# Up projection by seven products: sums of weights moved from GpSimd to accumulating transfers and VectorE, six plain pairs first

## The chip, the cores and the metric

The kernel runs on one core of one Trainium2 chip. It is a single program that computes all three blocks of the reference. The metric is device time in microseconds, the median of several runs. A core has five instruction queues: PE (TensorE, matrix products; PEld is its weight load), DVE (VectorE), ACT (ScalarE), POOL (GpSimd) and SP (SyncE, which here only issues transfers). Each works through its own instructions in order and waits on semaphores of the others.

## The reference

The input is x, 512 positions of 1024 features, fp32. Three blocks follow: an even mixer (differential attention and a chunked mLSTM), an odd mixer (spatial gating) and, after 16 meta tokens are put in front, a hybrid mixer (convolution and stick-breaking attention) with a gated feed-forward network. The change lies in the feed-forward network alone:

```
def conv_gated_mlp(xn, w_up_gate, conv_w_ffn, w_down):
    u, g = jnp.split(xn @ w_up_gate, 2, axis=-1)     # 1024 -> 2 x 2816
    u = causal_dwconv_2(u, conv_w_ffn)               # three taps over positions
    return (jax.nn.gelu(u) * g) @ w_down             # 2816 -> 1024
```

u and g are 2816 columns each, that is 22 blocks of 128 columns. Block m of u and block m of g make "pair" m; `act[m]` is gelu(conv(u)) * g of that pair.

## The kernel before, in words

Every fp32 operand of a product is split into a high part in fp32r and the remainder (hi by a cast on ACT, L77; lo by a subtraction on DVE, L78), and each product is three matmuls, hi*hi, hi*lo, lo*hi (`mm3`, L103 to L105). A weight block of 128 columns is loaded by one transfer on SP's queue (`load_w`, 512 KB, tile `wraw`, three buffers) and split into `whi` and `wlo` (three buffers each).

The up projection runs over the 22 pairs. The first `FIRST` pairs are plain: u and g are each 8 blocks of the inner dimension by two halves of 258 (or 254) positions, so 2 x 2 x 8 x 3 = 96 matmuls for a pair. Meanwhile the normalised input is combined for the later pairs: `xn` (L1367), the four sums `tq` (`seven_x`) and their split `sxh`, `sxl`.

The other pairs use a scheme of seven products (Strassen and Winograd): the weights of u and g, the two halves of the inner dimension, and the two halves of the positions make a 2 x 2 by 2 x 2 block product, done with 7 block products in place of 8, so 7 x 4 x 3 = 84 matmuls of 258 columns. `seven_w` forms the sums of weight blocks (`sa`, `sb`), `seven` issues the products into four PSUM tiles (`ps_sx`, `ps_sy`, `ps_sz`, `ps_sw`), keeps some of them in SBUF (`sn`, L173) and combines them to u and `act`. `conv_gelu` then applies the three taps (L1340, twice L1342), gelu (L1344), and POOL multiplies (L1377).

`residual` transposes the residual stream back to tokens (PE transposes `ps_h`, then four copies `ht` each on DVE); eight such calls are written into pairs 6 to 13, but a scheduler decides where they stand. The down projection follows (`ps_d`), whose input splits (`xl<-act`) may stand in the up projection already.

The program is put in order by a scheduler with a cost model of its own; the order on each engine is then fixed. It is the order that the chip runs, so it is shown below as it was built. In PE's order the pairs follow each other; only four matmuls of the first two products of pair m+1 stand ahead of the last two products of pair m.

Of the kernel before, what the change touches and what calls it, by code (L numbers as in the profile page):

```python
# [8 lines left out]
F32 = mybir.dt.float32  # L9
F32R = mybir.dt.float32r  # L10
BF16 = mybir.dt.bfloat16
AF = mybir.ActivationFunctionType
# [22 lines left out]
def kernel(ctx: ExitStack, tc: tile.TileContext, a, out):  # L35
# [84 lines left out]

    HK = KT // 2

    def add(o, x_, y_, op=ALU.add, eng=None):
        return (eng or G).tensor_tensor(o, x_, y_, op=op)

    def seven_w(pool, r1, r2):

        sa = pool.tile([128, KT, 128], F32, tag="sa", name="sa", bufs=4)  # L130
        sb = pool.tile([128, KT, 128], F32, tag="sa", name="sb", bufs=4)
        lo, hi = slice(0, HK), slice(HK, KT)
        add(sb[:, lo], r2[:, lo], r2[:, hi])
        add(sa[:, lo], sb[:, lo], r1[:, lo], ALU.subtract)
        add(sa[:, hi], r1[:, lo], r2[:, lo], ALU.subtract)
        add(sb[:, hi], r1[:, hi], sa[:, lo], ALU.subtract)
        w = {}
        for raw, names in ((r1, "12"), (sa, "67"), (sb, "53"), (r2[:, hi], "4")):
            sp_ = split_w(raw)
            for i, nm in enumerate(names):  # L140
                w[nm] = [x_[:, i * HK:(i + 1) * HK] for x_ in sp_]
        return w

    def seven_x(pool, tmp, p, xa, xb, n, out):

        tq = tmp.tile([128, 4, n], F32, tag="tq", name="tq")
        h0, h1 = slice(0, n), slice(n, 2 * n)
        t1, t2, t3, t4 = (tq[:, i] for i in range(4))
        add(t1, xa[:, h1], xa[:, h0], ALU.subtract)
        add(t3, xb[:, h1], xa[:, h1], ALU.subtract)  # L150
        add(t2, xb[:, h1], t1, ALU.subtract)
        add(t4, xb[:, h0], t2, ALU.subtract)
        for src, names in ((xa[:, h0], "1"), (xb, "23"), (tq.rearrange("p a b -> p (a b)"), "5674")):
            sp_ = [pool.tile([128, n * len(names)], F32R, tag=f"sx{names}{r}{p}", name=f"sx{r}") for r in "hl"]
            split(src, *sp_)
            for i, nm in enumerate(names):
                out[nm, p] = [x_[:, i * n:(i + 1) * n] for x_ in sp_]

    def seven(sw, sx, n, snp, o11, o12, o21, o22):

        bank = {}

        def product(nm, b, start):
            if start:
                bank[b] = pst("mm", n, f"ps_s{b}")
            wh, wl = sw[nm]
            for k in range(HK):
                mm3(bank[b], wh[:, k], wl[:, k], *sx[nm, k], start and k == 0, k == HK - 1, **kw)
            return bank[b]

        def keep(ps):
            t_ = snp.tile([128, n], F32, tag="sn", name="sn", bufs=5)
            A.copy(t_, ps)  # L173
            return t_

        s1 = keep(product("1", "x", True))
        add(o11, product("2", "y", True), s1, eng=V)
        u2 = keep(product("6", "x", False))
        s7 = keep(product("7", "w", True))
        u4 = keep(product("5", "x", False))  # L180
        add(o12, product("3", "z", True), u4, eng=V)
        n22, n21 = o22.shape[1], o21.shape[1]
        add(o22, u4[:, n - n22:], s7[:, n - n22:])
        add(o21, product("4", "w", False)[:, n - n21:], u2[:, n - n21:], eng=V)


    def ctile(shape, dt=F32, name="c"):
# [55 lines left out]
    def pv(name, i):  # L243
        c = col0[name] + i
        return pcol[:, c:c + 1]
# [1072 lines left out]
    with ExitStack() as ff:  # L1318
# [18 lines left out]

        def conv_gelu(m, u):
            cv = fp.tile([128, S], F32, tag="cv", name="cv")
            V.tensor_scalar(cv, u[:, 4:], pv("conv_w_ffn_2", 44 + m), None, op0=ALU.mult)  # L1340
            for tp in (1, 2):
                V.scalar_tensor_tensor(cv, u[:, 4 - tp:NQ - tp], pv("conv_w_ffn_2", (2 - tp) * 22 + m), cv,  # L1342
                                       op0=ALU.mult, op1=ALU.add)
            last["gelu"] = A.activation(cv, cv, AF.Gelu_apprx_tanh)  # L1344
            return cv


        FIRST = 4
        fx = tc.alloc_tile_pool(name="fx", bufs=1, reuse_waits="tile")
        ft = tc.alloc_tile_pool(name="ft", bufs=1, side="right", reuse_waits="tile")  # L1350
        sx = {}
        for m in range(FIRST):
# [9 lines left out]
                V.tensor_tensor(act[m][:, c0 - 4:c1 - 4], ps, rb[:, c0:c1], op=ALU.mult)  # L1362
            G.tensor_tensor(act[m], act[m], cv, op=ALU.mult)
            xn = []
            for i in (m, m + HK):
                xn.append(ft.tile([128, NQ], F32, tag="xn", name="xn", bufs=2))
                V.scalar_tensor_tensor(xn[-1], h[i], pv("g_pre_ffn_2", i), rb[:, :NQ], op0=ALU.mult, op1=ALU.mult)  # L1367
            seven_x(fx, ft, m, *xn, HQ, sx)
        ft.release()
        hr.release()  # L1370
        fw = tc.alloc_tile_pool(name="fw", bufs=2, side="right", reuse_waits="tile")
        for m in range(FIRST, 22):
            u = fp.tile([128, NQ], F32, tag="u", name="u")
            sw = seven_w(fw, *(load_w(wu, 0, KT, c + m * 128, 128) for c in (0, FF)))
            seven(sw, sx, HQ, fw, u[:, :HQ], u[:, HQ:], act[m][:, :HQ - 4], act[m][:, HQ - 4:])
            cv = conv_gelu(m, u)
            G.tensor_tensor(act[m], act[m], cv, op=ALU.mult)  # L1377
            if 6 <= m < 14:
                residual(m - 6)
# [68 lines left out]
```

## Time and profile before

| | |
|---|---|
| median of 3 runs | 2025.62 us (2025.27 to 2027.39) |
| profiled execution, its own time | 2026.93 us |
| its span in the trace | 2025.3 us |
| busy share of the span: PE, PEld, DVE, ACT, POOL | 97%, 88%, 67%, 50%, 21% |
| mean granted clock of TensorE | 0.992 |
| moved by transfers | 181.35 MB |

Busy times of the page are shares of the whole span. The up projection with its 22 pairs lies between about 1613 and 1898 us, and only there do the instructions of the two programs differ. The page's view in 40 slices shows it as the slices 33 to 37; the other views were read for that stretch alone. A duration in a timeline reaches to the end of the instruction's write; the next one often starts some 0.07 us before it, so the distance from start to start is what an instruction costs a queue that is full.

### The profile page before, as it was taken

The numbers are of one execution on the slowest core, as the hardware profiler recorded it, in microseconds if no ns is written. First come the engines' busy times: TensorE is split into PE (matmuls) and PEld (weight loads), VectorE is DVE, ScalarE is ACT, GpSimd is POOL, SyncE is SP. The second block draws the span as 40 slices with busy tenths as digits, with TensorE's granted clock in tenths as the row PEclk, the third lists the DMA queues.
The fourth block names the chain that finished last, engine by engine and source line by source line (L and its number), as shares of the span: only waits on it lengthen the run. The fifth ranks groups of instructions, "written<-read, shape, count | busy, mean of one in ns | idle before, by whom it ended". The sixth has DMA issues, their size and how long they took to land.

```text
span 2025.3 us, 33104 instructions
## 1 busy us (share of the span) xinstructions
PE 1972.7 (97%) x13182; PEld 1788.7 (88%) x13182; DVE 1364.5 (67%) x2181; ACT 1019.7 (50%) x1935; POOL 418.1 (21%) x437
## 2 busy tenths in 40 slices
PE   8999999999999999999999999999999997889998
PEld 6999988888899888889899999999999997888886
DVE  6676767668662666665877767676344598999634
ACT  5555566668664633364645544444223544444322
POOL 1011000000030111102422112110011157888300
PEclk9999999999999999999999999999999998999999
DMA  6223322222533333233312122223333332332322
GB/s 180 71 74 78 94 74 73 73 64 72 170 104 94 87 96 88 92 134 113 89 42 64 54 63 63 63 63 118 92 94 94 103 118 67 90 94 85 125 94 73
DMA packets 260664, 181.35 MB, mean 90 GB/s; under 512 B 8866, under 2 KB 245631, under 8 KB 260511
## 3 DMA queue, kind: packets, MB, share of 16 engines
q1 hardware_dynamic: 259455, 179.21, 29.7%
q8 instruction: 103, 1.69, 0.3%
q14 instruction: 50, 0.41, 0.1%
q10 hardware_dynamic: 1056, 0.04, 0.0%
HBM read 168.59 MB, written 10.63 MB: 88 GB/s over the span
## 4 chain that ended last, share of the span: by engine, by line
PE 85%; DVE 10%; issue 2%; ACT 2%; POOL 1%; DMA 1%; DVEq 0%; ACTq 0%; POOLq 0%
PE ps L103 13%; PE ps L105 13%; PE ps L104 13%; PE ps_v L103 5%; PE ps_v L105 5%; PE ps_v L104 5%; PE ps_o L103 3%; PE ps_o L104 3%; PE ps_o L105 3%; DVE wlo L78 2%; PE ps_d L103 2%; PE ps_d L105 2%; PE ps_d L104 2%; PE ps_z L1094 2%; PE ps_o L1174 1%
## 5 line engine op out<-in xcount | busy, mean ns | idle before, releaser
L77 ACT CAST whi<-wraw 128x1024 fp32r<-128x1024 f32 (+2 forms) x315 | 306.9, 979 | 407.8 <-PE ps L104 169.9
L78 DVE TENSOR_TENSOR wlo<-wraw,whi 128x1024 fp32r<-128x1024 f32 (+2 forms) x315 | 389.8, 1243 | 172.5 <-ACT whi L77 170.6
L104 PE MATMUL ps<-xl,whi 128*128 128x258 f32 (+3 forms) x1536 | 492.4, 322 | 3.8 <-DVE xl L82 3.8
L103 PE MATMUL ps<-xh,whi 128*128 128x258 f32 (+3 forms) x1536 | 491.7, 324 | 1.1 <-ACT whi L77 0.4
L105 PE MATMUL ps<-xh,wlo 128*128 128x258 f32 (+3 forms) x1536 | 491.1, 321 | 0.0
L104 PEld LDWEIGHTS ps<-xl,whi 128*128 128x128 f32 x1536 | 290.3, 189 | 28.9 <-DVE xl L82 5.8
L103 PEld LDWEIGHTS ps<-xh,whi 128*128 128x128 f32 x1536 | 288.2, 189 | 26.3 <-issue 1.2
L105 PEld LDWEIGHTS ps<-xh,wlo 128*128 128x128 f32 x1536 | 289.7, 189 | 24.0 <-issue 0.5
L103 PE MATMUL ps_v<-whi,xh 128*128 128x256 f32 x896 | 254.1, 285 | 3.1 <-ACT xh L81 2.7
L105 PE MATMUL ps_v<-whi,xl 128*128 128x256 f32 x896 | 253.5, 285 | 1.4 <-DVE xl L82 1.1
L104 PE MATMUL ps_v<-wlo,xh 128*128 128x256 f32 x896 | 253.7, 284 | 0.0
L103 PEld LDWEIGHTS ps_v<-whi,xh 128*128 128x128 f32 x896 | 169.1, 189 | 6.5 <-ACT xh L81 4.5
L105 PEld LDWEIGHTS ps_v<-whi,xl 128*128 128x128 f32 x896 | 169.5, 190 | 3.4 <-DVE xl L82 2.6
L104 PEld LDWEIGHTS ps_v<-wlo,xh 128*128 128x128 f32 x896 | 170.0, 190 | 1.5 <-issue 0.2
L105 PE MATMUL ps<-hi,wlo 128*128 128x258 f32 x384 | 108.6, 283 | 0.0
L103 PE MATMUL ps<-hi,whi 128*128 128x258 f32 x384 | 107.7, 282 | 0.0
L105 PE MATMUL ps_sx<-sxh,wlo 128*128 128x258 f32 x216 | 63.8, 295 | 20.8 <-DVE wlo L78 20.7
L961 DVE TENSOR_TENSOR t<-ps,rbc 128x258 f32<-128x258 f32 (+1 forms) x96 | 40.3, 424 | 64.1 <-PE ps L105 63.7
L104 PE MATMUL ps_o<-xl,whi 128*128 128x512 f32 x192 | 75.6, 394 | 0.0
L103 PE MATMUL ps_o<-xh,whi 128*128 128x512 f32 x192 | 75.4, 395 | 0.0
L105 PE MATMUL ps_o<-xh,wlo 128*128 128x512 f32 x192 | 74.5, 394 | 0.0
L105 PEld LDWEIGHTS ps<-hi,wlo 128*128 128x128 f32 x384 | 72.6, 189 | 0.0
(576 smaller groups left out, 4540.5 us busy)
## 6 DMA issues: line engine op xcount, KB each, us to landing
wraw<-in_l_w_in_dram SPq DMA_DIRECT2D x112, 512.0 KB
wraw<-in_w_in_dram SPq DMA_DIRECT2D x64, 512.0 KB
wraw<-in_w_up_gate_dram SPq DMA_DIRECT2D x44, 512.0 KB
wraw<-in_l_w_out_dram SPq DMA_DIRECT2D x24, 512.0 KB
wraw<-in_w_down_dram SPq DMA_DIRECT2D x22, 512.0 KB
wraw<-in_l_w_out_dram SPq DMA_DIRECT2D x16, 256.0 KB
wraw<-in_w_proj_attn_dram SPq DMA_DIRECT2D x8, 512.0 KB
wraw<-in_w_proj_conv_dram SPq DMA_DIRECT2D x8, 512.0 KB
```

The costliest lines, as they stand in the source:

```text
L77: A.copy(hi, src)
L78: V.tensor_tensor(lo, src, hi.bitcast(F32), op=ALU.subtract)
L103: T.matmul(ps, lhsT=ah, rhs=bh, start=first, stop=False, **kw)
L104: T.matmul(ps, lhsT=ah, rhs=bl, start=False, stop=False, **kw)
L105: T.matmul(ps, lhsT=al, rhs=bh, start=False, stop=last, **kw)
L961: V.tensor_tensor(dst[:, i * hn:(i + 1) * hn], ps, rb[:, c0 + i * hn:c0 + (i + 1) * hn], op=ALU.mult)
L1094: T.matmul(ps, lhsT=m_, rhs=x_[:, c0:c0 + n], start=False, stop=False, **kw)
L1174: T.matmul(po[:, n0:], lhsT=l_[:, b, hh:hh + 2, :].rearrange("p a d -> p (a d)"), rhs=a_[r_][:, c0:c0 + S - n0], start=po_first[0], stop=F ...
```

## The change

The two sums `sb` = sa + r1 are formed on DVE (L140, L141 after); `sa` is formed by transfers: for each half one plain transfer of 256 KB on SP's queue and then one transfer of 256 KB issued by POOL that adds its data to what lies in `sa` (L135, L136). Signs and the names of the sums are arranged so that two additions do in place of four operations with subtractions. Only the upper half of the g weights is still loaded by itself (`r2`, 256 KB). The sums `tq` of `seven_x` (L154 to L157) and the output block `o22` (L188) go from POOL to DVE; `o22` reads PSUM directly. The first tap of the convolution goes from DVE to ACT (L1346). `FIRST` goes from 4 to 6; the inputs' sums are still formed in the first four pairs. `sn` gets six buffers, `sa` two and `sb` one (four for both together before), and `dynamic_dma_scratch_size` goes from 1024 to 2048.

```diff
--- before.py
+++ after.py
@@ -120,36 +120,41 @@
 
 
 
+
     HK = KT // 2
 
-    def add(o, x_, y_, op=ALU.add, eng=None):
-        return (eng or G).tensor_tensor(o, x_, y_, op=op)
-
-    def seven_w(pool, r1, r2):
-
-        sa = pool.tile([128, KT, 128], F32, tag="sa", name="sa", bufs=4)
-        sb = pool.tile([128, KT, 128], F32, tag="sa", name="sb", bufs=4)
+    def seven_w(pool, w, c1, c2):
+
         lo, hi = slice(0, HK), slice(HK, KT)
-        add(sb[:, lo], r2[:, lo], r2[:, hi])
-        add(sa[:, lo], sb[:, lo], r1[:, lo], ALU.subtract)
-        add(sa[:, hi], r1[:, lo], r2[:, lo], ALU.subtract)
-        add(sb[:, hi], r1[:, hi], sa[:, lo], ALU.subtract)
-        w = {}
-        for raw, names in ((r1, "12"), (sa, "67"), (sb, "53"), (r2[:, hi], "4")):
+
+        def block(h, c):
+            return w[h * HK * 128:(h + 1) * HK * 128, c:c + 128].rearrange("(k p) c -> p k c", p=128)
+
+        sa = pool.tile([128, KT, 128], F32, tag="sa", name="sa", bufs=2)
+        for half, h, c in ((lo, 1, c2), (hi, 0, c1)):
+            nc.sync.dma_start(sa[:, half], block(0, c2))
+            G.dma_start(sa[:, half], block(h, c), accum_op=ALU.add)
+        r1 = load_w(w, 0, KT, c1, 128)
+        r2 = load_w(w, HK, HK, c2, 128)
+        sb = pool.tile([128, KT, 128], F32, tag="sb", name="sb", bufs=1)
+        V.tensor_tensor(sb[:, lo], sa[:, lo], r1[:, lo], op=ALU.add)
+        V.tensor_tensor(sb[:, hi], sb[:, lo], r1[:, hi], op=ALU.add)
+        w_ = {}
+        for raw, names in ((r1, "12"), (sb, "63"), (sa, "57"), (r2, "4")):
             sp_ = split_w(raw)
             for i, nm in enumerate(names):
-                w[nm] = [x_[:, i * HK:(i + 1) * HK] for x_ in sp_]
-        return w
+                w_[nm] = [x_[:, i * HK:(i + 1) * HK] for x_ in sp_]
+        return w_
 
     def seven_x(pool, tmp, p, xa, xb, n, out):
 
         tq = tmp.tile([128, 4, n], F32, tag="tq", name="tq")
         h0, h1 = slice(0, n), slice(n, 2 * n)
         t1, t2, t3, t4 = (tq[:, i] for i in range(4))
-        add(t1, xa[:, h1], xa[:, h0], ALU.subtract)
-        add(t3, xb[:, h1], xa[:, h1], ALU.subtract)
-        add(t2, xb[:, h1], t1, ALU.subtract)
-        add(t4, xb[:, h0], t2, ALU.subtract)
+        V.tensor_tensor(t1, xa[:, h0], xa[:, h1], op=ALU.subtract)
+        V.tensor_tensor(t3, xa[:, h1], xb[:, h1], op=ALU.subtract)
+        V.scalar_tensor_tensor(t2, xb[:, h1], -1.0, t1, op0=ALU.mult, op1=ALU.subtract)
+        V.tensor_tensor(t4, xb[:, h0], t2, op=ALU.add)
         for src, names in ((xa[:, h0], "1"), (xb, "23"), (tq.rearrange("p a b -> p (a b)"), "5674")):
             sp_ = [pool.tile([128, n * len(names)], F32R, tag=f"sx{names}{r}{p}", name=f"sx{r}") for r in "hl"]
             split(src, *sp_)
@@ -169,19 +174,20 @@
             return bank[b]
 
         def keep(ps):
-            t_ = snp.tile([128, n], F32, tag="sn", name="sn", bufs=5)
+            t_ = snp.tile([128, n], F32, tag="sn", name="sn", bufs=6)
             A.copy(t_, ps)
             return t_
 
         s1 = keep(product("1", "x", True))
-        add(o11, product("2", "y", True), s1, eng=V)
-        u2 = keep(product("6", "x", False))
+        V.tensor_tensor(o11, product("2", "y", True), s1, op=ALU.add)
+        v2 = keep(product("6", "x", False))
         s7 = keep(product("7", "w", True))
-        u4 = keep(product("5", "x", False))
-        add(o12, product("3", "z", True), u4, eng=V)
+        x5 = product("5", "x", False)
+        v4 = keep(x5)
         n22, n21 = o22.shape[1], o21.shape[1]
-        add(o22, u4[:, n - n22:], s7[:, n - n22:])
-        add(o21, product("4", "w", False)[:, n - n21:], u2[:, n - n21:], eng=V)
+        V.tensor_tensor(o22, s7[:, n - n22:], x5[:, n - n22:], op=ALU.subtract)
+        V.tensor_tensor(o12, product("3", "z", True), v4, op=ALU.add)
+        V.tensor_tensor(o21, product("4", "w", False)[:, n - n21:], v2[:, n - n21:], op=ALU.subtract)
 
 
     def ctile(shape, dt=F32, name="c"):
@@ -1337,7 +1343,7 @@
 
         def conv_gelu(m, u):
             cv = fp.tile([128, S], F32, tag="cv", name="cv")
-            V.tensor_scalar(cv, u[:, 4:], pv("conv_w_ffn_2", 44 + m), None, op0=ALU.mult)
+            A.activation(cv, u[:, 4:], AF.Copy, scale=pv("conv_w_ffn_2", 44 + m))
             for tp in (1, 2):
                 V.scalar_tensor_tensor(cv, u[:, 4 - tp:NQ - tp], pv("conv_w_ffn_2", (2 - tp) * 22 + m), cv,
                                        op0=ALU.mult, op1=ALU.add)
@@ -1345,7 +1351,7 @@
             return cv
 
 
-        FIRST = 4
+        FIRST = 6
         fx = tc.alloc_tile_pool(name="fx", bufs=1, reuse_waits="tile")
         ft = tc.alloc_tile_pool(name="ft", bufs=1, side="right", reuse_waits="tile")
         sx = {}
@@ -1362,16 +1368,17 @@
                 V.tensor_tensor(act[m][:, c0 - 4:c1 - 4], ps, rb[:, c0:c1], op=ALU.mult)
             G.tensor_tensor(act[m], act[m], cv, op=ALU.mult)
             xn = []
-            for i in (m, m + HK):
+            for i in (m, m + HK) if m < HK else ():
                 xn.append(ft.tile([128, NQ], F32, tag="xn", name="xn", bufs=2))
                 V.scalar_tensor_tensor(xn[-1], h[i], pv("g_pre_ffn_2", i), rb[:, :NQ], op0=ALU.mult, op1=ALU.mult)
-            seven_x(fx, ft, m, *xn, HQ, sx)
+            if xn:
+                seven_x(fx, ft, m, *xn, HQ, sx)
         ft.release()
         hr.release()
         fw = tc.alloc_tile_pool(name="fw", bufs=2, side="right", reuse_waits="tile")
         for m in range(FIRST, 22):
             u = fp.tile([128, NQ], F32, tag="u", name="u")
-            sw = seven_w(fw, *(load_w(wu, 0, KT, c + m * 128, 128) for c in (0, FF)))
+            sw = seven_w(fw, wu, m * 128, FF + m * 128)
             seven(sw, sx, HQ, fw, u[:, :HQ], u[:, HQ:], act[m][:, :HQ - 4], act[m][:, HQ - 4:])
             cv = conv_gelu(m, u)
             G.tensor_tensor(act[m], act[m], cv, op=ALU.mult)
@@ -1434,7 +1441,7 @@
     import concourse.bacc as _bacc
     from concourse.bass_utils import run_bass_kernel_spmd as _run
 
-    nc = _bacc.Bacc("TRN2", target_bir_lowering=False, num_devices=1, dynamic_dma_scratch_size=1024)
+    nc = _bacc.Bacc("TRN2", target_bir_lowering=False, num_devices=1, dynamic_dma_scratch_size=2048)
     arrays, aps = {}, {}
     for name in _INS:
         arr = _np.ascontiguousarray(inputs[name])
```

DVE's order in the steady part, from the end of pair 10's u to that of pair 11, in the kernel before (`sa_19425` and `sb_19426` belong to pair 11, `wraw_19275` to pair 10, `wraw_19421` to pair 11):

```order
L78 TENSOR_TENSOR wlo_19296<-wraw_19275,whi_19295 128x512
L1342 SCALAR_TENSOR_TENSOR cv_19255<-u_19128,pcol_84,cv_19255 128x512 x2
L78 TENSOR_TENSOR wlo_19432<-wraw_19421,whi_19431 128x1024
L78 TENSOR_TENSOR wlo_19436<-sa_19425,whi_19435 128x1024
L126 TENSOR_TENSOR u_19272<-ps_sz_19371,sn_19369 128x258
L126 TENSOR_TENSOR act10_17821<-ps_sw_19342,sn_19340 128x254
L78 TENSOR_TENSOR wlo_19440<-sb_19426,whi_19439 128x1024
L1340 TENSOR_SCALAR cv_19399<-u_19272,pcol_84 128x512
```

The same place on DVE in the changed kernel (`sa_19411` and `wraw_19418` belong to pair 11, `sa_19557`, `wraw_19562` and `sb_19566` to pair 12):

```order
L188 TENSOR_TENSOR act10_17821<-sn_19345,ps_sx_19289 128x258
L189 TENSOR_TENSOR u_19260<-ps_sz_19362,sn_19359 128x258
L190 TENSOR_TENSOR act10_17821<-ps_sw_19332,sn_19330 128x254
L140 TENSOR_TENSOR sb_19566<-sa_19557,wraw_19562 128x512
L78 TENSOR_TENSOR wlo_19432<-sa_19411,whi_19431 128x1024
L182 TENSOR_TENSOR u_19410<-ps_sy_19454,sn_19452 128x258
L1348 SCALAR_TENSOR_TENSOR cv_19389<-u_19260,pcol_84,cv_19389 128x512
L141 TENSOR_TENSOR sb_19566<-sb_19566,wraw_19562 128x512
L78 TENSOR_TENSOR wlo_19436<-wraw_19418,whi_19435 128x512
L1348 SCALAR_TENSOR_TENSOR cv_19389<-u_19260,pcol_84,cv_19389 128x512
L78 TENSOR_TENSOR wlo_19570<-wraw_19562,whi_19569 128x1024
L78 TENSOR_TENSOR wlo_19574<-sb_19566,whi_19573 128x1024
```

The sums of pair 12 now stand in DVE's queue directly before the split of pair 11's `sa`, and the first of them waits for the adding transfer into the `sa` of pair 12.

POOL's order at that place in the kernel before:

```order
L1377 TENSOR_TENSOR act9_17820<-act9_17820,cv_19255 128x512
L126 TENSOR_TENSOR act10_17821<-sn_19369,sn_19355 128x258
L126 TENSOR_TENSOR sb_19570<-wraw_19567 128x512
L126 TENSOR_TENSOR sa_19569<-wraw_19565,wraw_19567 128x512
L126 TENSOR_TENSOR sa_19569<-sb_19570,wraw_19565 128x512
L126 TENSOR_TENSOR sb_19570<-wraw_19565,sa_19569 128x512
L1377 TENSOR_TENSOR act10_17821<-act10_17821,cv_19399 128x512
```

And in the changed kernel:

```order
L136 DMA sa_19557<-in_w_up_gate_2_dram 128x4x128 x2
L1384 TENSOR_TENSOR act9_17820<-act9_17820,cv_19243 128x512
L136 DMA sa_19703<-in_w_up_gate_2_dram 128x4x128 x2
L1384 TENSOR_TENSOR act10_17821<-act10_17821,cv_19389 128x512
L136 DMA sa_19849<-in_w_up_gate_2_dram 128x4x128 x2
```

Of six arithmetic operations for a pair one is left on POOL, and two issues of transfers stand beside it; each pair's issues wait for the plain transfers into the same buffer.

## Rows read from the trace of the kernel before

**Rows 1.** Page, 40 slices of the span: busy tenths, granted clock.

```profile
PE   8999999999999999999999999999999997889998
...
DVE  6676767668662666665877767676344598999634
...
POOL 1011000000030111102422112110011157888300
PEclk9999999999999999999999999999999998999999
```

**Rows 2.** Stretches: us, busy (instructions) PE PEld DVE ACT POOL, PEclk, DMA share, GB/s.

```profile
1639.34:1664.82 25.48, 25.48 (x215) 25.48 (x214) 25.48 (x37) 9.54 (x14) 17.04 (x14) 1.00 0.32 93
1664.82:1702.26 37.44, 27.53 (x176) 25.21 (x175) 33.87 (x61) 15.22 (x24) 24.62 (x18) 0.77 0.28 89
1702.26:1897.00 194.74, 174.20 (x1374) 169.50 (x1372) 182.52 (x163) 88.26 (x150) 155.63 (x95) 0.98 0.31 92
1897.00:2025.30 128.30, 121.56 (x525) 98.12 (x523) 50.90 (x63) 39.30 (x64) 2.81 (x2) 0.99 0.28 94
```

**Rows 3.** Same view, pairs of seven products, fourth and last of eleven.

```profile
1773.59:1785.29 11.70, 10.44 (x87) 10.18 (x86) 11.17 (x11) 5.28 (x9) 9.20 (x7) 1.00 0.31 90
...
1856.57:1868.28 11.71, 10.44 (x87) 10.18 (x85) 11.14 (x12) 5.28 (x9) 8.27 (x6) 1.00 0.38 108
```

**Rows 4.** Waits, 1702.26 to 1868.28 us: waiter, releaser, total us, times, longest.

```profile
PE ps_sx L105 <- DVE wlo L78: 16.9, 12, 2.2
```

**Rows 5.** DVE and POOL timelines, two pairs: start, us, engine, line, operation, tile.

```profile
1781.80 1.59 DVE L1340 TENSOR_SCALAR cv<-u,pcol 128x512 f32<-128x512 f32 x1
...
1783.66 1.45 DVE L78 TENSOR_TENSOR wlo<-wraw,whi 128x512 fp32r<-128x512 f32 x1
1785.03 3.47 DVE L1342 SCALAR_TENSOR_TENSOR cv<-u,pcol,cv 128x512 f32<-128x512 f32 x2
...
1781.82 1.29 POOL L126 TENSOR_TENSOR sb<-wraw 128x512 f32<-128x512 f32 x1 [1.13 <-DMA wraw<-in_w_up_gate_dram]
...
1792.46 1.21 DVE L78 TENSOR_TENSOR wlo<-sb,whi 128x1024 fp32r<-128x1024 f32 x1
1793.60 0.47 DVE L1340 TENSOR_SCALAR cv<-u,pcol 128x512 f32<-128x512 f32 x1
1793.99 0.42 DVE L126 TENSOR_TENSOR u<-ps_sy,sn 128x258 f32<-128x258 f32 x1
1794.33 0.68 DVE L78 TENSOR_TENSOR wlo<-wraw,whi 128x512 fp32r<-128x512 f32 x1
1794.93 3.51 DVE L1342 SCALAR_TENSOR_TENSOR cv<-u,pcol,cv 128x512 f32<-128x512 f32 x2
...
1794.89 1.29 POOL L126 TENSOR_TENSOR sb<-wraw 128x512 f32<-128x512 f32 x1 [2.41 <-DMA wraw<-in_w_up_gate_dram]
```

**Rows 6.** Tiles cv and act: times, duration ns min/median/max, first and last start.

```profile
L1342 DVE SCALAR_TENSOR_TENSOR cv<-u,pcol,cv x44: 735/1667/1804, 1643.8 to 1901.0; 128x512 f32<-128x512 f32 x44
...
L1344 ACT ACTIVATE cv<-cv x22: 624/631/644, 1648.9 to 1901.8; 128x512 f32<-128x512 f32 x22
...
L1377 POOL TENSOR_TENSOR act<-act,cv x18: 1280/1556/2297, 1705.3 to 1902.6; 128x512 f32<-128x512 f32 x18
```

**Rows 7.** SP and POOL timelines around one load of weights.

```profile
1766.20 0.37 SPq L87 DMA_DIRECT2D wraw<-in_w_up_gate_dram  x1
...
1769.96 1.37 POOL L126 TENSOR_TENSOR sb<-wraw 128x512 f32<-128x512 f32 x1 [0.98 <-DMA wraw<-in_w_up_gate_dram]
```

**Rows 8.** Stretch of that load's packets (columns as in rows 2).

```profile
1767.20:1769.50 2.30, 2.30 (x21) 2.30 (x21) 2.30 (x4) 1.51 (x3) 1.78 (x2) 1.00 0.78 228
```

**Rows 9.** Stretches within the first three pairs of seven products.

```profile
1664.82:1673.90 9.08, 4.86 (x34) 3.84 (x32) 9.08 (x17) 3.30 (x6) 4.95 (x5) 1.00 0.50 174
1673.90:1691.00 17.10, 11.41 (x49) 10.16 (x50) 15.59 (x35) 6.54 (x12) 11.27 (x8) 0.50 0.11 33
```

**Rows 10.** DVE timeline: copies of the residual.

```profile
1673.30 1.66 DVE L1334 COPY ht<-ps_h 128x128 f32<-128x128 f32 x8
```

## Prediction

> **What bounds the kernel now.** I read the page first. Its slices show PE at 9 tenths throughout except slices 33 to 36, where it falls to 7 and 8 while DVE stands at 8 and 9 and POOL at 5 to 8 [rows 1]; there lie the pairs of seven products. A table of stretches then gives the stage's account [rows 2]. In the plain pairs (1639.34 to 1664.82 us) PE is busy all of 25.48 us, 215 instructions, 0.1185 us each. From 1664.82 to 1897.00, the 18 pairs of seven, pass 232.2 us: 37.4 in the first stretch, at a mean clock of 0.77, and 194.7 in the second, where DVE is busy 182.5. The rest, 128.3 us, is the down projection and the end, which the change doesn't touch.
>
> One pair in the steady part takes 11.70 us, of which PE works 10.44 and DVE 11.17 [rows 3]. The waits name who is late: PE stands before the first product of the next pair for DVE's `wlo`, 12 times, 16.9 us in all [rows 4]. DVE's timeline says why DVE takes so long [rows 5]. While POOL computes, a `wlo` of 128x512 takes 1.37 us from start to start (1783.66 to 1785.03), and the first tap lasts 1.59. In the one pair where POOL waited 2.41 us for a load, up to 1794.89, the same two were 0.60 and 0.47, and the next two taps were slow again. The taps' fastest and median times, 735 and 1667 ns, say the same [rows 6]. So the bound is DVE, and much of its time is lost beside POOL's arithmetic.
>
> **What the change does to a steady pair.** All times are start to start. DVE loses the first tap. It gains two sums of 128x512 and `o22`. Undisturbed that makes three splits of 128x1024 at 1.14 (1792.46 to 1793.60), three operations of 128x512 at 0.60, two taps at 0.67 (735 ns less the overlap of 0.07), and four of 128x258 at 0.34: 3.42 + 1.80 + 1.34 + 1.36 = 7.9 us [rows 5, 6]. Of POOL's six operations only the product with gelu stays, 1.28 to 1.56 us [rows 6]; if DVE stood still for all of it, DVE would need 9.5. PE's 84 matmuls are 84 x 0.1185 = 10.0 us, and today's busy time of a pair is 10.44. PE becomes the bound; I take 10.4 for a pair. ACT gets the first tap at the price of a gelu, 0.63 [rows 6], on 5.28 busy of 11.70 [rows 3]: it is hidden.
>
> DVE's place in the order matters more than its sum. The sums of pair m+2 stand in its queue before the split of `sa` of pair m+1. So DVE now waits for the adding transfer, and behind that wait stand the split of `sa`, which PE needs for products 5 and 7, and everything after it. `sa` has two buffers: the loads into the buffer of pair m start when its split is done. The loop is: semaphore to SP, 0.2 assumed; plain load of 256 KB; adding transfer (call it a, from POOL's release to DVE's start); sum 0.60; split of the next `sa` 1.14. For 512 KB, SP's issue at 1766.20 freed POOL at 1769.96, 3.76 us, of which the packets took 2.3 [rows 7, 8]; 256 KB is then 2.6. The pair's time is at least 4.5 + a, and the adding transfer is hidden as long as a stays below 5.9.
>
> No row shows an adding transfer or one issued by POOL, so I bound a. Below: as a plain load of its size, 2.6. If it has to read and write, its packets double: 3.76, like 512 KB. What the issue costs POOL no row shows either; the nearest is any operation of its own, 1.3 to 1.6, which makes 5.3. Above: it shares the queues with the 512 KB of `r1` that are issued at about that time, 2.3 more, 7.6. I take 5.3, the row nearest to what it does; the ends give a pair of 10.4 (hidden) and of 12.1.
>
> The Trainium skill, "DMA: Bandwidth & Descriptors", section "Anatomy of one DMA — SWDGE (gpsimd) path", gives 2.0 us plus bytes / 436e3 for a transfer issued by GpSimd; for 256 KB that is an estimate of 2.6, hidden by over 3 us. Its formula gives 3.2 for 512 KB, where the trace shows 3.76, so it is short even for a plain load. Against the change speaks the Trainium skill, "Collectives: The Full Stack", "The bandwidth ceiling": an add in the transfer needs two reads and ran at half the rate of a copy. No run here shows that; by it the packets' part of a doubles, as I assumed.
>
> The queues carry 1.84 MB for a pair in place of 1.05 MB. 228 GB/s came at a share of 0.78 [rows 8], so 1.84 MB fill the engines for 6.3 us, and 8.1 with the added bytes counted twice, of 10.4. That is loaded, not full.
>
> **Plain pairs and start.** Pairs 4 and 5 become plain: 192 matmuls x 0.1185 = 22.8 us. Their DVE work is small (no sums of the input), so DVE, which today is late at 1664.82, catches up while PE is busy. The sums of the input, 16 of 128x258, 0.34 each by the nearest row [rows 5], go to DVE in the first four pairs; by its order DVE then meets PE's results on time. The start of the sevens keeps a price: some 30 copies of the residual, 0.2 each (1.66 for eight) [rows 10], and five splits of `act` at 0.60 stand in DVE's queue in pairs 6 and 7, 9 us against 1.3 spare in each of two pairs; about 6.5 late, and PE's transposes and the last loads before them add one or two: 8 us. Today's start loses 37.4 - 176 x 0.1185 = 16.6, with 17.1 us at half the clock (0.50, the 1.2 GHz level) after PE had worked 4.9 of 9.1 us [rows 9]. Bounds for the new start are 3 and 17.
>
> **Sum.** 22.8 + 16 x 10.4 + 8 = 197.2 us in place of 232.2: 35 less. The profiled execution took 2026.93 us, 1.6 over its span and 1.3 over the median shown; 2025.62 - 35.0 = 1990.6, so 1991.
>
> **Rivals.**
> - The adding transfer is the new wait (0.20). With a = 7.2 a pair takes 11.7, as today; 22.8 + 187.2 + 8 = 218.0, which gives 2011. For it: the loads of a pair come together, and a has only 0.6 us to spare on my value. Against it: 512 KB need but 3.76 today.
> - The start stays as bad as now, half the clock included (0.10): 17 in place of 8 gives 2000. For it: DVE's pile of copies. Against it: two plain pairs in which DVE catches up.
> - DVE stays the bound (0.06), because POOL's two issues hold it as POOL's arithmetic does: 7.9 + 3 x 1.56 = 12.6, a stage of 232, 2025, no change. For it: in rows 5 any work of POOL slows DVE. Against it: an issue need not read what DVE reads, and no row shows one.
> - Slower (0.10): the adding transfer is far dearer than any row suggests, because an issue of 512 runs of 512 bytes occupies POOL, or the addition the queues, for 8 us. It decides from a pair of (232.2 - 30.8) / 16 = 12.6 on, that is a = 8.1; at a = 8.5 a pair takes 13.0, the stage 239, and the kernel 2032. For it: no row bounds that work from above. Against it: POOL has nothing else to do but one product for each pair.
>
> **Numbers.** The forecast has 0.54. Its own range is 1981 (pairs of 10.1, a start of 3) to 1998. 1981 to 2014 takes in the bad start and most of the waiting case; left out are the slower case, DVE as the bound and the tails. 0.2% is 4 us, about what a measurement of this kernel can tell from no change: the first three cases make faster 0.84, the slower one 0.10, and the DVE case, 2025, falls on all three sides: faster 0.86, within 0.03, slower 0.11.
>
> **What would show it.** After the change, pairs should follow each other at 10.2 to 10.6 us with PE waiting under 0.5 in each; the tap's median should fall from 1667 ns to near 735; DVE should idle one to two us in a pair; the time from POOL's issue to DVE's sum should be 4 to 6 us. The sevens should begin near 1690 and the down projection near 1862. I am wrong if DVE's longest wait is for the adding transfer into `sa` and PE's for `wlo` of `sa` behind it, if DVE is still busy 95% there, or if the clock falls to 0.50 again at the start.

## The result and the profile after

The changed kernel takes 2041.01 us (median of 4 runs, 2039.55 to 2042.85), the kernel before 2025.59 beside it: 1.0075 times as long, 95% interval 1.0057 to 1.0092. The forecast was 1991, at least 1981 and at most 2014. It was wrong: the kernel became slower.

Three stretches of the changed kernel, cut at the same events as [rows 2] (the plain pairs' second part, the sevens, the rest; columns as there):

```profile
1639.34:1687.70 48.36, 48.36 (x407) 48.36 (x406) 44.62 (x77) 22.07 (x31) 11.65 (x6) 1.00 0.36 104
1687.70:1912.81 225.11, 185.79 (x1380) 181.27 (x1378) 164.90 (x222) 102.71 (x164) 61.61 (x47) 0.92 0.65 138
1912.81:2041.14 128.33, 121.60 (x525) 98.12 (x523) 50.68 (x63) 40.03 (x65) 1.30 (x1) 0.98 0.29 95
```

The plain part grew by 48.36 - 25.48 = 22.9 us, as forecast (22.8), and the rest is unchanged. The whole miss lies in the sevens: 225.1 us for 16 pairs, where the forecast had 174.4. Neither engine fills that time: PE is busy 186 us of it and DVE 165. From one pair's first combination (L182) to the next pass 13.5 us (median; 11.75 before).

The waits of that stage, 1690 to 1912 us (waiter, releaser, total us, times, longest), and the taps' durations (ns min/median/max):

```profile
POOL sa L136 <- issue: 83.4, 18, 6.4
POOL sa L136 <- DMA sa<-in_w_up_gate_dram: 50.6, 10, 6.1
...
PE ps_sw L105 <- DVE wlo L78: 29.9, 13, 4.4
...
DVE wlo L78 <- ACT whi L77: 22.8, 15, 3.0
DVE sb L140 <- issue: 19.1, 8, 4.1
...
DVE sb L140 <- DMA sa<-in_w_up_gate_dram: 13.4, 4, 5.0
```

```profile
L1348 DVE SCALAR_TENSOR_TENSOR cv<-u,pcol,cv x44: 734/739/2797, 1641.2 to 1916.7; 128x512 f32<-128x512 f32 x44
```

PE's long waits are no longer at `ps_sx` [rows 4] but at `ps_sw`, products 5 and 7, whose weights are the split of `sa`. DVE's longest waits are before the sum L140, 32.5 us in its two lines. The profile names the adding transfer in four of the twelve; by the trace's landings the sum starts within 0.1 us after that transfer has landed in all but one of the 16 pairs. These are the signs that the prediction named for being wrong. The part on the taps came true: 739 ns in place of 1667 [rows 6].

One cycle in the timelines of SP, POOL and DVE (start, us, engine, line, operation, tile; in brackets the idle time before it):

```profile
1785.85 0.93 SPq L135 DMA_DIRECT2D sa<-in_w_up_gate_dram  x2
1788.05 2.17 SPq L87 DMA_DIRECT2D wraw<-in_w_up_gate_dram  x2
...
1782.11 1.30 POOL L136 DMA_DIRECT2D sa<-in_w_up_gate_dram  x1 [4.69 <-issue]
1782.89 1.84 POOL L1384 TENSOR_TENSOR act<-act,cv 128x512 f32<-128x512 f32 x1
1789.60 1.30 POOL L136 DMA_DIRECT2D sa<-in_w_up_gate_dram  x1 [4.86 <-DMA sa<-in_w_up_gate_dram]
1795.35 1.30 POOL L136 DMA_DIRECT2D sa<-in_w_up_gate_dram  x1 [4.45 <-issue]
1796.13 1.81 POOL L1384 TENSOR_TENSOR act<-act,cv 128x512 f32<-128x512 f32 x1
...
1782.48 3.35 DVE L78 TENSOR_TENSOR wlo<-sa,whi 128x1024 fp32r<-128x1024 f32 x1
...
1795.11 0.69 DVE L140 TENSOR_TENSOR sb<-sa,wraw 128x512 f32<-128x512 f32 x1 [2.57 <-DMA sa<-in_w_up_gate_dram]
1795.72 3.31 DVE L78 TENSOR_TENSOR wlo<-sa,whi 128x1024 fp32r<-128x1024 f32 x1
```

The loop through `sa`'s two buffers can be read off. The split ends at 1785.83; SP issues the plain loads at once; POOL issues the adding transfer at 1789.60 (3.8 later); DVE's sum starts at 1795.11 (5.5 later); the next split starts at 1795.72 (0.6) and takes 3.3: together 13.2 us, the time of a pair. Over the stage the medians of the four legs are 3.76, 5.64, 0.61 and 3.31, 13.3 in all. Two things stand out. The split is slow exactly while POOL's product with gelu (L1384) runs, in 12 of the 16 pairs; in the other four it takes 1.2 us. And the product runs just then because the second adding issue stands ahead of it in POOL's queue: it goes out only at 1795.35, when the first transfer has landed, after a wait for which the profile names nothing ("issue").

### The profile page after: what moved, and what is told of

Its sections match the earlier page's. It is cut to its first block, busy times and chain, and to the rows that moved or that the text cites. A ratio compares the mean times of both kernels' runs of the same rounds, so it can differ in the third digit from the quotient of the medians.

```text
span 2041.1 us, 33265 instructions
## 1 busy us (share of the span) xinstructions
PE 1979.1 (97%) x13206; PEld 1797.6 (88%) x13206; DVE 1331.9 (65%) x2221; ACT 1033.2 (51%) x1945; POOL 291.7 (14%) x363
## 4 chain that ended last, share of the span: by engine, by line
PE 86%; DVE 6%; DMA 4%; issue 3%; ACT 1%; POOL 0%; DVEq 0%; POOLq 0%; ACTq 0%
PE ps L103 14%; PE ps L105 14%; PE ps L104 14%; PE ps_v L103 5%; PE ps_v L105 5%; PE ps_v L104 5%; DMA sa<-in_w_up_gate_dram 3%; PE ps_o L103 3%; PE ps_o L104 3%; PE ps_o L105 3%; PE ps_d L103 2%; PE ps_d L105 2%; PE ps_d L104 2%; PE ps_z L1100 2%; PE ps_o L1180 1%
## 5 line engine op out<-in xcount | busy, mean ns | idle before, releaser
L104 PE MATMUL ps<-xl,whi 128*128 128x258 f32 (+3 forms) x1600 | 510.4, 320 | 3.6 <-DVE xl L82 3.4
L103 PE MATMUL ps<-xh,whi 128*128 128x258 f32 (+3 forms) x1600 | 509.9, 323 | 1.6 <-ACT xh L81 0.9
L105 PE MATMUL ps<-xh,wlo 128*128 128x258 f32 (+3 forms) x1600 | 509.2, 320 | 0.0
L78 DVE TENSOR_TENSOR wlo<-wraw,whi 128x1024 fp32r<-128x1024 f32 (+2 forms) x315 | 369.6, 1178 | 170.3 <-ACT whi L77 168.5
L104 PEld LDWEIGHTS ps<-xl,whi 128*128 128x128 f32 x1600 | 302.6, 189 | 28.6 <-DVE xl L82 5.6
L103 PEld LDWEIGHTS ps<-xh,whi 128*128 128x128 f32 x1600 | 300.1, 189 | 26.8 <-ACT xh L81 1.7
L105 PEld LDWEIGHTS ps<-xh,wlo 128*128 128x128 f32 x1600 | 301.9, 189 | 24.0 <-issue 0.5
L103 PEld LDWEIGHTS ps<-hi,whi 128*128 128x128 f32 x384 | 72.4, 189 | 0.0
```

Of the source, the lines that this page charges most:

```text
L78: V.tensor_tensor(lo, src, hi.bitcast(F32), op=ALU.subtract)
L103: T.matmul(ps, lhsT=ah, rhs=bh, start=first, stop=False, **kw)
L104: T.matmul(ps, lhsT=ah, rhs=bl, start=False, stop=False, **kw)
L105: T.matmul(ps, lhsT=al, rhs=bh, start=False, stop=last, **kw)
```

## The experiments

Each was timed against the kernel before on the same chip. "Pair" is the median distance of L182 from pair to pair, read from each trace.

| run | edit | us | ratio to before (95%) | pair, us |
|---|---|---|---|---|
| after | the change | 2041.0 | 1.0075 (1.0057 to 1.0092) | 13.5 |
| e1_scr2176 | 2176 bytes for descriptors | 2009.1 | 0.9918 (0.9903 to 0.9933) | 11.6 |
| e2_sa3 | three buffers of `sa` | 2013.3 | 0.9939 (0.9924 to 0.9954) | 11.5 |
| e3_multV | gelu product on DVE | 2014.5 | 0.9944 (0.9929 to 0.9958) | 11.6 |
| e9_scr_multV | e1 and e3 | 2010.0 | 0.9922 (0.9905 to 0.9938) | 11.6 |
| e10_scr_sa3 | e1 and e2 | 2005.7 | 0.9898 (0.9883 to 0.9913) | 11.5 |
| e5_all3 | e1, e2 and e3 | 1994.0 | 0.9842 (0.9826 to 0.9859) | 10.2 |
| e6_copy | plain copies for adding ones | 1996.1 | 0.9854 (0.9839 to 0.9869) | 10.5 |
| e4_sumsV | all sums on DVE | 1990.7 | 0.9828 (0.9812 to 0.9844) | 10.2 |
| e11_sumsV_multV | e4 and e3 | 1990.5 | 0.9822 (0.9808 to 0.9837) | 10.2 |
| e8_sumsV4 | e4 with four plain pairs | 2001.4 | 0.9883 (0.9868 to 0.9897) | 10.2 |
| e7_bfirst6 | before, six plain pairs | 2012.2 | 0.9933 (0.9918 to 0.9948) | 11.75 |

The scheduler might have answered an edit with another order. It hardly did: in e1 and e6 every engine's order in this stage is that of the changed kernel; with the product on DVE one tap changes its place, with three buffers some copies of the residual, splits of `act`, loads and a few matmuls do.

**e1_scr2176.**

```diff
-dynamic_dma_scratch_size=2048
+dynamic_dma_scratch_size=2176
```

> The changed kernel with 2176 bytes of room for the descriptors of GpSimd's transfers in place of 2048; nothing else. In the changed kernel a pair takes 13.4 us, and the second adding transfer of a pair is issued only when the first has landed (an issue of 4.45 us that waits for nothing that the profile shows), so that the gelu product of GpSimd starts with the split of sa and the split takes 3.31 us in place of 1.2. Theory A (the loop through the two buffers of sa: 3.8 us to the adding issue, 5.5 for the adding transfer, 0.6 for the sum, 3.3 for the split): with room for both transfers the second is issued at once, its issue takes under 1.5 us, the product runs beside the wait and not beside the split, the split falls to 1.2 to 2 us and the pair to 11 to 12 us: 2005 to 2022 us in all. Theory B (the transfer engines are too full, busy 0.6 to 0.76 of the stage): two adding transfers in flight at once only make each other slower, the pair stays at 13 to 13.5 us: 2037 to 2043 us. If the size has nothing to do with the late second issue: no change at all, 2041 us.

POOL's timeline in one cycle, and DVE beside it:

```profile
1774.31 2.63 POOL L136 DMA_DIRECT2D sa<-in_w_up_gate_dram  x2 [7.50 <-DMA sa<-in_w_up_gate_dram]
1775.89 2.38 POOL L1384 TENSOR_TENSOR act<-act,cv 128x512 f32<-128x512 f32 x1
...
1775.42 3.93 DVE L78 TENSOR_TENSOR wlo<-sb,whi 128x1024 fp32r<-128x1024 f32 x1 [0.79 <-ACT whi L77]
...
1780.88 1.21 DVE L78 TENSOR_TENSOR wlo<-sa,whi 128x1024 fp32r<-128x1024 f32 x1
```

128 bytes more and both adding transfers go out together: theory A's numbers held. The product now meets another split, that of `sb`, and slows it instead; `sa`'s takes 1.21. The loop's legs are 3.66, 6.12, 0.61 and 1.22, 11.6 in all. The slowed split of `sb` has brought DVE near the same time: in four of the last eleven pairs the sum starts 0.6 to 0.8 us after the landing, in the others at once.

**e2_sa3.**

```diff
-sa = pool.tile([128, KT, 128], F32, tag="sa", name="sa", bufs=2)
+sa = pool.tile([128, KT, 128], F32, tag="sa", name="sa", bufs=3)
```

> The changed kernel with three buffers for sa in place of two; nothing else. Theory A (the loop through the buffers of sa of 13.2 us bounds a pair): the plain load and the adding transfers of a pair begin one pair earlier, the loop allows 13.2 x 2/3 or less for a pair, TensorE or VectorE bounds it at 10.4 to 11.2 us, and the longest wait of VectorE for the adding transfer (50.6 us of GpSimd, 13.4 us of VectorE in the stage) goes: 1993 to 2005 us. Theory B (the transfer engines are too full): the pair stays near 13 us and the time at 2035 to 2041 us. Theory C (VectorE and GpSimd disturb each other, VectorE is the bound): 12.5 us a pair, 2027 us.

8 us above theory A's range and below the others', with a pair of 11.5: none of the three theories has it. With the loop eased DVE waits for `r1` instead (tile `wraw`; waits 1700 to 1900 us), and the product meets the sum L140 (timelines of DVE and POOL):

```profile
DVE sb L140 <- DMA wraw<-in_w_up_gate_dram: 14.9, 11, 2.2
```

```profile
1785.00 2.11 DVE L140 TENSOR_TENSOR sb<-sa,wraw 128x512 f32<-128x512 f32 x1 [1.50 <-DMA wraw<-in_w_up_gate_dram]
...
1783.93 1.29 POOL L136 DMA_DIRECT2D sa<-in_w_up_gate_dram  x1 [5.26 <-issue]
1784.71 1.84 POOL L1384 TENSOR_TENSOR act<-act,cv 128x512 f32<-128x512 f32 x1
1788.80 1.30 POOL L136 DMA_DIRECT2D sa<-in_w_up_gate_dram  x1 [2.25 <-DVE u L182]
1795.07 1.31 POOL L136 DMA_DIRECT2D sa<-in_w_up_gate_dram  x1 [4.98 <-issue]
```

But the adding transfers now also follow one another without a break: in the trace each is issued 0.3 us after the one before it has landed, so that two of them, 11.1 us from 1783.93 to 1795.07, nearly fill a pair by themselves. Which of the two waits holds e2 at 11.5 is open; three buffers with the product on DVE and 2048 bytes were not run.

**e3_multV.**

```diff
-            G.tensor_tensor(act[m], act[m], cv, op=ALU.mult)
+            V.tensor_tensor(act[m], act[m], cv, op=ALU.mult)
```

> The changed kernel with the gelu product of the pairs by seven products on VectorE in place of GpSimd; nothing else. Theory A: the product no longer starts beside the split of sa, the split falls from 3.31 to 1.2 us, 2.1 us of the loop of 13.2 go, VectorE carries 0.7 us more: pair 11.1 to 11.8 us, 2007 to 2018 us. Theory B (transfer engines too full): the loop is set by transfers, pair 12.8 to 13.4 us, 2032 to 2041 us. Theory C (the two engines disturb each other, VectorE is the bound): the pair falls to 11 us as in theory A, but VectorE is then busy over nine tenths of it and never waits for the adding transfer.

As theory A has it. Without the product on POOL the split of `sa` takes 1.22 us, and DVE waits for the adding transfer (the tile's splits, 1700 to 1870 us; waits, 1700 to 1900):

```profile
L78 DVE TENSOR_TENSOR wlo<-sa,whi x15: 1207/1218/1224, 1699.7 to 1866.6; 128x1024 fp32r<-128x1024 f32 x15
```

```profile
DVE sb L140 <- DMA sa<-in_w_up_gate_dram: 34.6, 11, 3.7
```

The legs are 4.78, 5.10, 0.61 and 1.22, 11.7.

**e4_sumsV.** r1 and r2 are loaded whole, and DVE forms all four sums.

```diff
-        for half, h, c in ((lo, 1, c2), (hi, 0, c1)):
-            nc.sync.dma_start(sa[:, half], block(0, c2))
-            G.dma_start(sa[:, half], block(h, c), accum_op=ALU.add)
-        r2 = load_w(w, HK, HK, c2, 128)
+        r2 = load_w(w, 0, KT, c2, 128)
+        V.tensor_tensor(sa[:, lo], r2[:, lo], r2[:, hi], op=ALU.add)
+        V.tensor_tensor(sa[:, hi], r2[:, lo], r1[:, lo], op=ALU.add)
```

> The changed kernel without adding transfers: r1 and r2 are loaded whole as before the change (512 KB each), and all four sums of weights are formed by VectorE; six plain pairs, the other sums and everything else as changed. Theory A (the adding transfers' loop is what costs): no loop through sa is left but loads of 3.8 us that run ahead, VectorE gets 2 sums of 0.6 to 0.7 us more per pair (about 10.2 us of work), TensorE 10.4: pair 10.4 to 11.0 us, 1992 to 2003 us. Theory B (the transfer engines are too full): 1.0 MB plain per pair in place of 1.25 MB with adding ones also frees them, so the same; it differs from A only together with the three buffers. Theory C (VectorE bound and disturbed): pair 11.7 to 12.5 us, 2015 to 2028 us.

1990.7 us, under the lower end expected. In the steady part PE is busy throughout, and DVE has room with all four sums (columns as in [rows 2]):

```profile
1730.00:1850.00 120.00, 120.00 (x989) 119.64 (x988) 108.50 (x166) 71.90 (x118) 23.16 (x12) 1.00 0.35 105
```

So the adding transfers bought 1.2 us of DVE's time for each pair where DVE was not the bound.

**e5_all3.** The three edits of e1, e2 and e3 together.

> The changed kernel with all three edits of the first batch at once: 2176 bytes for the descriptors, three buffers of sa, the gelu product on VectorE; the adding transfers stay. Alone, each of the three left a pair at 11.4 to 11.7 us, with another wait each. Theory A (one loop, of which each edit takes a different piece): together they take the loop off the path, TensorE bounds a pair at 10.2 to 10.7 us, TensorE's waits in the stage fall under 5 us: 1990 to 1999 us. Theory B (behind the loop stands a floor of the transfers: their engines were busy 0.73 to 0.75 of a pair of 11.5 us in all three): the pair stays at 11.2 to 11.6 us, 2006 to 2013 us, and VectorE's longest wait is for a transfer.

Theory A: the adding transfers stay, a pair takes 10.2 us, and PE is busy all the time although the transfer engines are at 0.82 (steady part, then all 16 pairs):

```profile
1720.00:1850.00 130.00, 130.00 (x1069) 129.21 (x1068) 111.02 (x169) 79.16 (x128) 30.13 (x24) 1.00 0.82 169
1687.71:1864.20 176.49, 170.71 (x1380) 168.99 (x1379) 145.69 (x237) 101.47 (x164) 41.53 (x32) 0.98 0.83 177
```

A floor of the transfers at 11.5 us is excluded; so are full transfer engines as the cause.

**e6_copy.** This kernel leaves out the addition in the transfers.

```diff
-            G.dma_start(sa[:, half], block(h, c), accum_op=ALU.add)
+            G.dma_start(sa[:, half], block(h, c))
```

> The changed kernel with the 32 adding transfers of GpSimd as plain copies of the same 256 KB (they overwrite the plain load; the addition of the two blocks is left out). Theory A1 (it is the addition in the transfer that costs: its packets took 2.6 us for 256 KB, 2.4 times as long for a byte as a plain load's, and both transfers together do not fit the room for descriptors): packets 1.1 to 1.6 us, from issue to landing 3.5 to 4.2 us in place of 4.9, the second issue no longer waits, pair 10.8 to 11.7 us, 2000 to 2014 us. Theory A2 (it is GpSimd's queue and the order, whatever the transfer does): from issue to landing 4.6 us or more, the second issue still waits, pair 12.6 to 13.4 us, 2028 to 2041 us.

The time and the pair fell below A1's range, though the median from issue to landing stayed at 4.9 us, which A1 had put at 3.5 to 4.2. The queues of the changed kernel and of this one, 1720 to 1850 us (packets, MB, share of the 16 engines' time):

```profile
q1 hardware_dynamic: 26076, 13.03, 35.5%
q0 software_dynamic: 10294, 5.11, 32.2%
```

```profile
q1 hardware_dynamic: 31561, 15.77, 42.8%
q0 software_dynamic: 1935, 6.33, 15.9%
```

For a MB the adding queue takes 6.3% and the plain one 2.7%, 2.3 times as much; as plain copies POOL's transfers take 2.5%, like SP's, although their packets are larger. Both issues go out together, 0.8 us apart, so the product is over before `sa`'s split (it meets that of `sb`, which takes 2.9). The legs are 3.73, 4.95, 0.60 and 1.22, 10.5 in all. Here the loop is not alone: DVE mostly goes into the sum without idle time, and PE is busy nearly throughout (stretch):

```profile
1720.00:1850.00 130.00, 129.04 (x1044) 126.67 (x1042) 117.63 (x150) 76.67 (x123) 34.06 (x36) 1.00 0.59 171
```

**e7_bfirst6.** The kernel before with the part of the change on plain pairs.

```diff
-        FIRST = 4
+        FIRST = 6
-            for i in (m, m + HK):
+            for i in (m, m + HK) if m < HK else ():
```

> The kernel before with six plain pairs in place of four (the input's sums still in the first four), nothing else: what that part of the change is worth by itself. Two pairs by seven products at 11.7 us go and two plain ones of 11.4 us come, and the sums of the input are done two pairs ahead of their use: 2018 to 2028 us if the sums of weights on GpSimd set the pair (the same time or a little less). If the start of the seven products was held up by those sums (the first pairs took 20.1 and 15.2 us), up to 11 us less: 2014 us.

13.2 us less (2025.4 - 2012.2) by this part alone, a little beyond the most that was expected for the start; the pair stays at 11.75, so the gain is the start's. The first 24.3 us of the sevens (stretch, columns as in [rows 2]):

```profile
1687.70:1712.00 24.30, 23.20 (x195) 22.99 (x194) 21.46 (x37) 9.93 (x17) 18.43 (x11) 1.00 0.48 152
```

PE stands nearly full at a granted clock of 1.00, where the kernel before had 17.1 us at 0.50 [rows 9].

**e8_sumsV4.** e4 with `FIRST = 4`.

> All four sums of weights on VectorE from whole loads, with four plain pairs in place of six. A pair by seven products took 10.21 us with six plain pairs, a plain one takes 11.4: 2.4 us less if the start is as before, 1988 us; but the sums of the input of the fourth plain pair then stand directly ahead of the first products on VectorE, which was busy all of the first 20 us of the sevens even with six plain pairs: up to 8 us more, 1996 us. Over 2000 us would mean that the six plain pairs carry much of the gain.

2001.4, over the line from which six plain pairs were to carry much of the gain: they are worth 2001.4 - 1990.7 = 10.7 us here too, while the steady pairs keep their 10.2. At the start the clock falls to its lower level again, after PE had worked 4.9 of 6.7 us (stretches, columns as in [rows 2]):

```profile
1664.10:1670.80 6.70, 4.88 (x39) 4.26 (x37) 6.70 (x18) 2.09 (x3) 1.33 (x1) 1.00 0.69 238
1670.80:1691.30 20.50, 8.71 (x36) 7.30 (x36) 18.20 (x43) 6.89 (x11) 0.00 (x0) 0.50 0.09 27
```

**e9_scr_multV and e10_scr_sa3.** Two edits of the three, to part what each leaves.

> The changed kernel with 2176 bytes for the descriptors and the gelu product on VectorE, but two buffers of sa: the loop through the buffers without the collision and without the late second issue. The loop is then the leg from the end of sa's split to the adding issue (3.8 us), the adding transfer (6.2 us from issue to landing where two are in flight), the sum (0.7), the split (1.2): 11.9 us for a pair, or 11.2 with 5.5 for the first transfer alone: 2004 to 2016 us, and VectorE's longest wait is for the adding transfer. Rival (the collision and the late issue were the whole of it, the buffers none): pair 10.3 to 10.6 us, 1993 to 1998 us.

> The changed kernel with 2176 bytes for the descriptors and three buffers of sa, the gelu product on GpSimd: the loop without the limit of two buffers, the collision left in. Loop theory: 15 us of loop over two pairs in flight leave 8 us, the collision costs VectorE 2 to 2.8 us of a pair, busy 10.3 us with it: TensorE and VectorE about even, pair 10.3 to 11.0 us, 1994 to 2005 us. Rival (VectorE stretched by GpSimd's product bounds it whatever the loop): pair 11.3 us or more, 2008 us or more.

In e9 the loop theory held: the collision is gone, two buffers remain, and DVE stands before the sum (DVE's timeline):

```profile
1774.93 0.41 DVE L190 TENSOR_TENSOR act<-ps_sw,sn 128x254 f32<-128x254 f32 x1
1778.27 0.69 DVE L140 TENSOR_TENSOR sb<-sa,wraw 128x512 f32<-128x512 f32 x1 [2.92 <-DMA sa<-in_w_up_gate_dram]
1778.88 1.22 DVE L78 TENSOR_TENSOR wlo<-sa,whi 128x1024 fp32r<-128x1024 f32 x1
```

In e10 the theory's range was missed by little, and the rival is nearer: the loop is off (the transfer lands 9 to 12 us before its sum), but with the collision DVE itself takes 11.5 us for a pair (stretch, then the timelines of DVE and POOL):

```profile
1720.00:1850.00 130.00, 120.52 (x970) 117.76 (x969) 120.46 (x137) 72.08 (x115) 46.82 (x35) 1.00 0.80 163
```

```profile
1774.04 3.96 DVE L78 TENSOR_TENSOR wlo<-sb,whi 128x1024 fp32r<-128x1024 f32 x1 [0.82 <-ACT whi L77]
...
1772.95 2.64 POOL L136 DMA_DIRECT2D sa<-in_w_up_gate_dram  x2 [7.55 <-DMA sa<-in_w_up_gate_dram]
1774.52 2.39 POOL L1384 TENSOR_TENSOR act<-act,cv 128x512 f32<-128x512 f32 x1
```

A split of 1.2 us grows to 4.0 around a product of 2.4, and DVE is busy 120.5 of 130 us.

**e11_sumsV_multV.** e4 with e3's edit.

> All four sums of weights on VectorE from whole loads, six plain pairs, and the gelu product of the later pairs on VectorE too; GpSimd does nothing in the pairs by seven products. With the product on GpSimd a pair is bound by TensorE at 10.21 us and VectorE is busy 8.3 us of it, so the steady pairs stay at 10.2 us; at the start, where VectorE was busy all of 20 us, 0.7 us a pair more against stretches of 1.1 us that go: 1988 to 1993 us. If GpSimd's product stretched operations on the path anywhere, up to 3 us less, 1987 us.

The same time as e4 within the intervals: where PE is the bound, the collision costs nothing. (DVE was busy 9.2 us of a pair in e4, not 8.3 as expected: 108.5 of 120 us in e4's stretch.)

## Why the prediction was wrong

**What held.** Two plain pairs cost 22.9 us (22.8 forecast). DVE stopped being the bound, and the tap fell to 739 ns. The adding transfer took 5.6 us from POOL's issue to DVE's sum; the prediction had taken a = 5.3 and called it hidden below 5.9. Where nothing is in PE's way (e5), a pair takes 10.2 us (10.4 forecast) and the kernel 1994 us (1991). The start then costs 176.5 - 16 x 10.24 = 12.7 us, between the 8 forecast and the rival's 17. A term that the forecast lacked lies there (e5, DVE's timeline): DVE stands before its first sum for the first adding transfer, and PE's longest wait, 3.7 us, ends with the cast of that sum's `sb`.

```profile
1695.06 0.69 DVE L140 TENSOR_TENSOR sb<-sa,wraw 128x512 f32<-128x512 f32 x1 [6.73 <-DMA sa<-in_w_up_gate_dram]
```

That a came out near 5.3 is partly luck. Its parts were 3.76, as for 512 KB, and 1.5 for the issue; by the same parts a plain copy would take 2.6 + 1.5 = 4.1 us, and it took 4.9 (e6).

**The step that failed** is the loop, "at least 4.5 + a": the 4.5 was mis-sized far more than a. It measured 3.76 + 0.61 + 3.31 = 7.7, so that with a = 5.6 a pair takes 13.3 us, and a would have been hidden only below 2.7. Two of its terms were too small.

- "Split of the next `sa` 1.14" measured 3.3. The prediction charged POOL's remaining product to DVE's sum (9.5 us, still below PE's 10.4) and did not ask which instruction the product would meet. It meets this split in 12 of the 16 pairs, since the second adding issue holds POOL until the first transfer has landed, and the same landing starts DVE's sum and split. e3 takes the product away, and the split is 1.22; e1 and e10 move it, and the split of `sb` grows instead. The Trainium skill, "SBUF — State Buffer", section "Who interferes with whom", says that an instruction of VectorE with two inputs in SBUF contends with one of GpSimd that reads SBUF, for a port pair that is an exclusive lock. The rows agree in size: 3.3 less 1.2 is 2.1, a little over the product's 1.8. The split had begun 0.4 us before the product (1782.48 and 1782.89) and was still the one that grew.
- Semaphore and plain load, "0.2" and "2.6", measured 3.8. In the trace's semaphore updates SP issues 0.03 us after the split, the load has landed 3.1 us later, and POOL's issue begins another 0.67 us later. That last piece had no term. (The prediction counts a from POOL's release; with the 0.67 in it a is 6.3, 1.0 over its price, and the other legs are 7.0, 2.5 over theirs.) The load itself has company: SP issues both halves within 0.9 us and `r1` behind them. Before, 512 KB took 3.76 from SP's issue to POOL's start [rows 7], which would have been the nearer row. That the company is the reason was not tried by itself.

The legs sum to 13.3 us after the change and to 11.6, 11.7, 11.6 and 10.5 in e1, e3, e9 and e6, as the pairs do. That alone shows nothing: the legs cut a period in four, and in e5, where PE is the bound, the distances between the same events also make a pair (3.8, 4.7, 0.6 and 1.2). Two other things show the loop. No leg has slack: after the change, in e3 and in e9 SP issues 0.03 us after the split's end, and from the sixth pair on POOL's issue begins 0.67 us after the plain load's landing and the sum 0.08 us after the adding transfer's, in every pair; in e5 the transfer lands about 9 us before its sum. And the period follows a leg: e3 shortens the split by 2.1 us and the pair by 1.9, and e5, which is e9 with a third buffer, takes the pair from 11.6 to 10.2.

So the loss has two parts: 1.4 us a pair over PE's 10.2 is the loop through two buffers with an undisturbed split (e3, e9), and 1.9 the collision that lies in it. They don't simply add up, since with the loop off the collision alone leaves a pair at 11.5 (e10). The stage is 225.1 - 176.5 = 48.6 us longer than e5's; the 14 distances of L182 after the first sum to 45 us more than e5's, and the first, at the start, is 5 longer. With two buffers the late second issue has no price of its own (e3 has it, e9 has not, both take 11.6); it sets what the product collides with.

**The rivals.** Two rivals named the right wait, the adding transfer, and the slower of them the right threshold, a pair over 12.6 us; but both made it of a longer a (7.2 and 8.1), where the rest of the loop was longer. DVE as the bound is refuted by its 165 busy us of 225. That an adding transfer's packets count double was about right: they took 2.3 times a plain one's time for a MB. The Trainium skill, "Collectives: The Full Stack", "The bandwidth ceiling", has an add at half a copy's rate, for the reducing step of a collective; the trace is near that. The fit in the Trainium skill, "DMA: Bandwidth & Descriptors", "Anatomy of one DMA — SWDGE (gpsimd) path", an estimate of 2.6 us for 256 KB, stands against a median of 4.8 us from issue to landing (5.5 for the first of a pair), and 4.9 even as a plain copy (e6), both beside other transfers.

**The clock.** The stage's mean granted clock was 0.92. It is not the cause: a cycle at 0.74 and the next one at 1.00 take the same time, from split to split of `sa` (stretches):

```profile
1769.10:1782.48 13.38, 10.01 (x63) 10.01 (x64) 10.15 (x14) 5.02 (x9) 3.90 (x4) 0.74 0.66 137
1782.48:1795.72 13.24, 12.58 (x105) 12.37 (x105) 10.17 (x13) 6.51 (x11) 3.93 (x4) 1.00 0.69 140
```

**A better version.** The change is worth keeping without its adding transfers: with six plain pairs, the first tap on ACT, the other sums as changed and all four sums of weights on DVE (e4) the kernel takes 1990.7 us, 0.9828 times the kernel before. The six plain pairs were parted from the rest (e7, e8); the tap and the other sums were not tried one by one.

## What to carry to other kernels

Before work is taken off an engine, add up what it will be bound by afterwards: DVE could have carried the two sums under PE's shadow, and a transfer in their place only opened a loop. In a loop through buffers every leg is priced as it will run, with the transfers that are issued beside it and the instruction of the other engine that the same event releases; a collision that is harmless in an engine's sum is paid in full on the loop. A loop may be read off a timeline in four numbers, but that they add up to the period proves nothing, since they cut it. A loop is shown when no leg has slack and when a run with a shorter leg has a shorter period.

## What the runs showed of the hardware

- Room for descriptors decided whether two adding transfers of 256 KB were in flight: with 2048 bytes the second issue stood up to 6.4 us for "issue", with 2176 both went out 0.8 us apart. As plain copies both fit in 2048.
- An adding transfer took 2.3 times the engines' time of a plain one for the same bytes, and POOL 1.30 us for an issue, against 0.79 for a plain copy (in both cases the next instruction starts 0.8 us after the issue's start).
- POOL's product took 1.30 us in e6, 1.84 after the change, a median of 1.92 in e4 and 2.4 in e1 and e10, where two adding issues lay directly ahead. In e1 the two issues and the product together take 3.96 us (1774.31 to 1778.27), about three times 1.30, so the longer records may hold the rest of the issues; in e4 no issue lies ahead. Neither was tried.
